# Layer 0's pooled rows and gates transposed on VectorE instead of through DRAM, the block writes moved to ScalarE's queue, and two output columns opened early, in a two-layer fp32 decoder trunk

## The chip, the cores and the metric

One Trainium2 chip, of which one core is used. The metric is the device time of one execution in microseconds (us). The engines are called PE (TensorE, the matmuls), PEld (its weight loads), DVE (VectorE), ACT (ScalarE), POOL (GpSimd) and SP (SyncE, which here only issues DMAs). A queue name such as SPq or ACTq is the DMA queue that this engine fills; an engine works through its instructions strictly in order, so one that waits holds up all behind it.

## The reference

256 positions of width 2048, one batch, all in fp32. What bears on the change is layer 0 and the way that layer 1 gets its queries:

```python
def pool_layer(x, mem, norm_g, w_in, w_pool, pool_scale, mem_g, w_mem_kv, w_out):
    h = rmsnorm(x, norm_g)
    u, zu, qm, zm = jnp.split(h @ w_in, [POOL_W, 2 * POOL_W, 2 * POOL_W + MEM_W], axis=-1)
    y_pool = multiscale_pool(u, w_pool, pool_scale) * jax.nn.silu(zu)
    y_mem = memory_attention(qm * HEAD_DIM ** -0.5, mem, mem_g, w_mem_kv) * jax.nn.silu(zm)
    return x + jnp.concatenate([y_pool, y_mem], axis=-1) @ w_out
```

`multiscale_pool` cuts the 1536 channels of u into four groups of 384. In group g each channel becomes its trailing mean over 2, 4, 8 or 16 positions minus the position's own value; then a 384x384 matrix per group mixes the channels and a scale per channel follows. Layer 1 projects queries, gates and memory queries out of the new stream, attends over compressed, selected and windowed keys (12 heads in four groups of three), mixes the branches and projects out.

## The kernel before, in words

**Products.** Every product is fp32 made of three passes: a number is split into a high part that the matmul keeps exactly (ACT casts it, L138 or L142) and the rest (DVE subtracts, L139 or L143), and `mm3` (L147 to L149) sums high by high, high by low and low by high. `project` (L168) multiplies the stream (stationary, transposed, two blocks of 128 positions) by a weight matrix. It goes in chunks of two k-tiles, 128 x 2 x 384 or 128 x 2 x 512 weights. A chunk is one load on SP's queue into a `raw` tile (four of them), one cast on ACT and one subtraction on DVE into a `w` tile (four of them), and 12 matmuls. After each chunk `project` calls `pump`, which advances the oldest generator of a queue of background work by one step; `flush` runs that queue empty.

**Order.** The source order is only a wish: a scheduler that works with its own price list sets the final order on every engine, and that order is fixed when the program runs.

**Transposes.** A projection leaves rows (positions on the partitions). Where channels must be on the partitions, `turned` (L116 to L128) does it in three steps: two DVE stream transposes turn every 32 x 32 block in place (tile `nt`, L121), one DMA on SP's queue writes `nt` to DRAM (`bnc`, L123), and four DMAs on SP's queue read the blocks back in their new places (tile `tt`, L127). The first waits for DVE, the other four wait until `bnc` has landed.

**Layer 0 around the change.** For each group g of four: project u (384 columns, 8 chunks), scale the rows (ACT, L230), turn; start the background work `pooled` (L465: shifted sums `pt` at L474 and L475, the mean at L481, its split `dd`); project the gate (8 chunks), SiLU (ACT, L236), turn; run `pooled` to its end (`flush(pl)`); start the background work `mixed` (L489: two pool weight loads, 27 matmuls into the PSUM tiles `mix`, and for each of three blocks `yf` at L501, which needs the turned gate). The 18 matmuls of the first two blocks go to one PSUM tile, the 9 of the third to another.

**Output projection of layer 0** (L536 to L550): four columns of 512, each 8 chunks. Column 0 multiplies the six chunks whose inputs are ready, flushes the queue, and then the last two. Each finished column is added to x (L547), turned, and split into layer 1's input `h1`.

**Layer 1**: for the groups 3, 0, 1, 2, `project_q` and `project_gate` (8 chunks each) put turned tiles into `qns` and `gns`; the generator `nsa_heads` (L680) takes them as soon as `ready` (L798) sees them, splits a head's query (`q<-tt`, ACT and DVE), and computes scores (`sc`), softmax, transposes and outputs.

Of the kernel before, what the change touches and what calls it, by code (L numbers as in the profile page):

```python
# [20 lines left out]
P = 128  # L21
# [44 lines left out]
def tile_trunk(ctx, tc, x, mem, xt, memt, positions, w_mem_kv, w_out, a_w_in, a_w_pool, b_w_in, w_kv, cmp_w1, cmp_w2,  # L66
# [22 lines left out]

    bg = deque()  # L90

    def pump():

        while bg:
            try:
                return next(bg[0])
            except StopIteration:
                bg.popleft()
# [17 lines left out]
    def turned(nat, n):  # L116


        nt = wk.tile([P, 4, 2, HD], F32, name="nt", tag="nat", bufs=5)[:, 0:n]
        for t in range(2):  # L120
            V.transpose(nt[:, :, t, :], nat[:, t, 0:n * HD].rearrange("p (h d) -> p h d", d=HD))  # L121
        d = dr.tile([8, P, HD], F32, name="bnc", tag="bnc", bufs=4)[0:2 * n]
        nc.sync.dma_start(d.rearrange("a p d -> p a d"), nt.rearrange("p h t d -> p (h t) d"))  # L123
        tt = wk.tile([P, 4, S], F32, name="tt", tag="nat", bufs=5)[:, 0:n]
        dv = d.rearrange("a (i r) (j c) -> j r (a i) c", r=32, c=32)
        for j in range(4):
            nc.sync.dma_start(tt[32 * j:32 * j + 32].rearrange("r h (i c) -> r (h i) c", c=32), dv[j])  # L127
        return tt  # L128

    def pst(name):  # L130
# [334 lines left out]
    def pooled(g, ut, ds_):  # L465

        def temp():
            return wk.tile([P, 928], F32, name="pt", tag="pm", bufs=2)

        win = POOL_WINDOWS[g]  # L470
        a = ut
        for sh in (1, 2, 4, 8)[:g + 1]:
            b = temp()[:, 0:768].rearrange("p (c s) -> p c s", c=3)
            V.tensor_copy(b[:, :, 0:sh], a[:, :, 0:sh])  # L474
            V.tensor_tensor(out=b[:, :, sh:S], in0=a[:, :, sh:S], in1=a[:, :, 0:S - sh], op=ALU.add)  # L475
            a = b
            yield
        fac = cst[:, C_FAC + 16 * g:C_FAC + 16 * g + win].unsqueeze(1).to_broadcast([P, 3, win])
        V.tensor_tensor(out=a[:, :, 0:win], in0=a[:, :, 0:win], in1=fac, op=ALU.mult)
        d = temp()[:, 0:768].rearrange("p (c s) -> p c s", c=3)  # L480
        V.scalar_tensor_tensor(d, a, 1.0 / win, ut, op0=ALU.mult, op1=ALU.subtract)  # L481
        dd = wk.tile([P, 1536], F32R, name="dd", tag="late", bufs=1)
        dd = [dd[:, 768 * i:768 * i + 768].rearrange("p (c s) -> p c s", c=3) for i in range(2)]
        yield
        split(*dd, d)
        ds_.append(dd)
        yield

    def mixed(g, sg, ds_):  # L489

        wpv = a_w_pool[0, g].rearrange("(a p) n -> p a n", p=P)
        wps = wload(wpv[:, 0:2, :]), wload(wpv[:, 2:3, :])
        yield
        ps = pst("mix")
        for b in range(3):
            o = ps[:, b * S:(b + 1) * S] if b < 2 else pst("mix")[:, 0:S]
            for c in range(3):
                mm3(o, [z[:, c % 2, b * P:(b + 1) * P] for z in wps[c // 2]], [z[:, c, :] for z in ds_[0]], c == 0, c == 2)
            k = 3 * g + b
            y = wk.tile([P, S], F32, name="yf", tag="yf", bufs=1)  # L500
            V.scalar_tensor_tensor(y, o, psc[:, k:k + 1], sg[:, b, :], op0=ALU.mult, op1=ALU.mult)  # L501
            A.copy(y0[k][0], y)
            G.tensor_tensor(out=y0[k][1], in0=y, in1=f32(y0[k][0]), op=ALU.subtract)
            yield

    for g in range(4):
        ut = turned(rows_scaled(project(a_w_in[0], 384 * g, 384, x0), rx, 384), 3)
        if g == 0:
            flush()
            later(rotary_tables())  # L510
        ds_ = []
        pl = later(pooled(g, ut, ds_))
        sg = turned(silu_gate(project(a_w_in[0], 1536 + 384 * g, 384, x0), rx, 384), 3)
        flush(pl)
        later(mixed(g, sg, ds_))

    h1d = dr.tile([S, D], F32, name="h1d")
# [11 lines left out]
    def h1_T(xr, c):  # L529
        yield  # L530
        for j in range(2):
            k = 4 * c + 2 * j
            two_T(xr, 2 * j, h1[k:k + 2])
            yield

    for c in range(4):  # L536
        n_ = slice(c * 512, (c + 1) * 512)
        if c == 0:
            pp = project(w_out[0], 0, 512, y0, groups=[6, 7, 0, 1, 2, 3], done=False)
            flush()  # L540
            pp = project(w_out[0], 0, 512, y0, groups=[4, 5], pp=pp)
        else:
            pp = project(w_out[0], c * 512, 512, y0)
        xr = natural()
# [135 lines left out]
    def nsa_heads():  # L680
# [115 lines left out]
        todo = [(g, h) for g in (3, 0, 1, 2) for h in range(3)]  # L796

        def ready(i, what):  # L798
            while i < len(todo) and todo[i][0] not in what:
                yield  # L800

        yield from ready(0, qns)
        qs[todo[0]] = q_T(qns[todo[0][0]], todo[0][1])
        yield
        for i in range(len(todo) + 1):
            if i < len(todo):
# [1 line left out]
            yield  # L808
            if i + 1 < len(todo):
                yield from ready(i + 1, qns)  # L810
                qs[todo[i + 1]] = q_T(qns[todo[i + 1][0]], todo[i + 1][1])
            if i:
                yield from ready(i - 1, gns)
                gt[todo[i - 1]] = gns[todo[i - 1][0]][:, todo[i - 1][1], :]
            yield
            if i:
                transposed(*todo[i - 1])
# [9 lines left out]
    def project_q(g):  # L827
# [8 lines left out]
                V.tensor_scalar(gc, gc, cst[:, C_RV + t:C_RV + t + 1], None, op0=ALU.mult)  # L836
        qn = rows_scaled(pq, r1, 384)
        rope(heads(qn, 3), 3, 0, 2)
        qns[g] = turned(qn, 3)

    def project_gate(g):
        gns[g] = turned(silu_gate(project(bw, 1572 + 384 * g, 384, h1, ng[1]), r1, 384), 3)

    for g in (3, 0, 1, 2):
        project_q(g)
# [120 lines left out]
```

## Time and profile before

| what | value |
|---|---|
| runs of the kernel, us | 875.3, 881.72, 882.1 (median 881.72) |
| the profiled execution, us | 875.92 |
| its span, first to last instruction, us | 874.1 |
| around the span, us | 1.8 |
| PE busy, share of the span | 849.9 us, 97% |
| DVE busy | 608.5 us, 70% |
| ACT busy | 539.6 us, 62% |
| mean granted PE clock | 0.994 of full |

A row of instructions in time order reads: start, duration (us), engine, line of the program, operation, output <- inputs, shapes, count, and in brackets the idle time of that engine before it and who ended it. "x2" with 1.03 us is two instructions that together took 1.03 us. A row of waits reads: engine and line that waited, who released it, total us, number of times, longest. Rows of stretches give the length, the busy time of every engine with its count, the granted PE clock, the busy share of the DMA engines and the rate in GB/s.

### The profile page before, as it was taken

The numbers are of one execution on the slowest core, as the hardware profiler recorded it, in microseconds if no ns is written. First come the engines' busy times: TensorE is split into PE (matmuls) and PEld (weight loads), VectorE is DVE, ScalarE is ACT, GpSimd is POOL, SyncE is SP. The second block draws the span as 40 slices with busy tenths as digits, with TensorE's granted clock in tenths as the row PEclk, the third lists the DMA queues.
The fourth block names the chain that finished last, engine by engine and source line by source line (L and its number), as shares of the span: only waits on it lengthen the run. The fifth ranks groups of instructions, "written<-read, shape, count | busy, mean of one in ns | idle before, by whom it ended". The sixth has DMA issues, their size and how long they took to land.

```text
span 874.1 us, 12967 instructions
## 1 busy us (share of the span) xinstructions
PE 849.9 (97%) x4408; PEld 752.4 (86%) x4408; DVE 608.5 (70%) x1261; ACT 539.6 (62%) x1025; POOL 40.2 (5%) x63
## 2 busy tenths in 40 slices
PE   9999999999999999999999999989999999999996
PEld 6888889999999878777888888869999989888786
DVE  6677556867565665457667878857689879887752
ACT  7877646755444454447566667747697868676641
POOL 0000000020101020000000000000000010001000
PEclk9999999999999999999999999999999999999999
DMA  9999978678777789898887786798777766786642
GB/s 311 345 274 288 306 222 192 180 219 225 216 204 226 222 257 269 262 262 268 241 228 205 201 276 227 238 251 226 213 193 208 172 183 153 213 244 223 214 159 96
DMA packets 236058, 199.14 MB, mean 228 GB/s; under 512 B 111576, under 2 KB 186328, under 8 KB 235992
## 3 DMA queue, kind: packets, MB, share of 16 engines
q1 hardware_dynamic: 234696, 195.55, 76.9%
q0 software_dynamic: 576, 2.10, 0.6%
q8 instruction: 34, 0.56, 0.3%
q10 hardware_dynamic: 720, 0.67, 0.2%
q14 instruction: 32, 0.26, 0.1%
HBM read 180.99 MB, written 17.30 MB: 227 GB/s over the span
## 4 chain that ended last, share of the span: by engine, by line
PE 60%; DMA 18%; DVE 9%; SPq 4%; ACT 4%; issue 4%; DVEq 0%; POOLq 0%; POOL 0%; ACTq 0%
PE pp L148 18%; PE pp L149 18%; PE pp L147 18%; DMA bnc<-nt 7%; SPq L127 4%; DMA raw<-in_w_out_dram 3%; DMA tt<-bnc 3%; DVE w L139 2%; DMA raw<-in_b_w_in_dram 2%; DVE w L143 1%; DVE nt L121 1%; PE hp L602 1%; DVE pt L475 1%; ACT w L142 1%; ACT pm L714 1%
## 5 line engine op out<-in xcount | busy, mean ns | idle before, releaser
L139 DVE SCALAR_TENSOR_TENSOR w<-raw,fst,w 128x512 fp32r<-128x512 f32 (+2 forms) x320 | 210.5, 699 | 52.7 <-ACT w L138 51.9
L143 DVE TENSOR_TENSOR w<-raw,w 128x1024 fp32r<-128x1024 f32 (+2 forms) x170 | 181.7, 1076 | 92.7 <-ACT w L142 91.1
L138 ACT ACTIVATE w<-raw,fst 128x512 fp32r<-128x512 f32 (+2 forms) x320 | 199.0, 675 | 64.8 <-PE pp L149 31.1
L142 ACT CAST w<-raw 128x1024 fp32r<-128x1024 f32 (+2 forms) x170 | 155.4, 923 | 130.1 <-PE pp L149 66.8
L148 PE MATMUL pp<-w,h1h 128*128 128x512 f32 (+2 forms) x512 | 187.4, 366 | 0.3 <-DVE w L139 0.3
L149 PE MATMUL pp<-w,h1l 128*128 128x512 f32 (+2 forms) x512 | 187.7, 367 | 0.0
L147 PE MATMUL pp<-w,h1h 128*128 128x512 f32 (+2 forms) x512 | 178.8, 367 | 3.0 <-ACT w L138 3.0
L148 PE MATMUL pp<-w,x0h 128*128 128x384 f32 (+1 forms) x320 | 111.2, 348 | 0.0
L149 PE MATMUL pp<-w,x0l 128*128 128x384 f32 (+1 forms) x320 | 111.0, 347 | 0.0
L147 PEld LDWEIGHTS pp<-w,h1h 128*128 128x128 f32 x512 | 96.2, 188 | 13.7 <-ACT w L138 3.8
L147 PE MATMUL pp<-w,x0h 128*128 128x384 f32 (+1 forms) x320 | 107.7, 348 | 0.0
L148 PEld LDWEIGHTS pp<-w,h1h 128*128 128x128 f32 x512 | 96.6, 189 | 10.9 <-DVE w L139 1.1
L149 PEld LDWEIGHTS pp<-w,h1l 128*128 128x128 f32 x512 | 96.6, 189 | 10.3
L148 PEld LDWEIGHTS pp<-w,x0h 128*128 128x128 f32 x320 | 60.5, 189 | 2.8 <-DVE w L143 0.3
L149 PEld LDWEIGHTS pp<-w,x0l 128*128 128x128 f32 x320 | 60.5, 189 | 2.5
L147 PEld LDWEIGHTS pp<-w,x0h 128*128 128x128 f32 x320 | 59.9, 189 | 2.6
L148 PE MATMUL pp<-w,y0h 128*128 128x512 f32 x128 | 50.2, 392 | 1.7 <-DVE w L143 1.7
L148 PE MATMUL pp<-w,mth 128*128 128x512 f32 x128 | 50.3, 393 | 0.1
L149 PE MATMUL pp<-w,mtl 128*128 128x512 f32 x128 | 50.0, 391 | 0.0
L149 PE MATMUL pp<-w,y0l 128*128 128x512 f32 x128 | 49.9, 390 | 0.0
L147 PE MATMUL pp<-w,y0h 128*128 128x512 f32 x128 | 48.7, 390 | 0.1
L147 PE MATMUL pp<-w,y1h 128*128 128x512 f32 (+1 forms) x128 | 46.0, 366 | 0.8 <-DVE nat L869 0.8
(287 smaller groups left out, 1219.8 us busy)
## 6 DMA issues: line engine op xcount, KB each, us to landing
raw<-in_w_out_dram SPq DMA_DIRECT2D x60, 512.0 KB, 5.2
raw<-in_a_w_in_dram SPq DMA_DIRECT2D x64, 384.0 KB, 3.9
raw<-in_w_kv_dram SPq DMA_DIRECT2D x48, 512.0 KB, 4.8
raw<-in_b_w_in_dram SPq DMA_DIRECT2D x56, 384.0 KB, 3.9
raw<-in_w_mem_kv_dram SPq DMA_DIRECT2D x31, 512.0 KB, 5.8
raw<-in_a_w_in_dram SPq DMA_DIRECT2D x16, 512.0 KB, 4.9
raw<-in_b_w_in_dram SPq DMA_DIRECT2D x16, 512.0 KB, 4.9
raw<-in_cmp_w_dram SPq DMA_DIRECT2D x16, 512.0 KB, 4.8
```

The costliest lines, as they stand in the source:

```text
L121: V.transpose(nt[:, :, t, :], nat[:, t, 0:n * HD].rearrange("p (h d) -> p h d", d=HD))
L127: nc.sync.dma_start(tt[32 * j:32 * j + 32].rearrange("r h (i c) -> r (h i) c", c=32), dv[j])
L138: A.activation(hi, src, AF.Copy, scale=scale)
L139: V.scalar_tensor_tensor(lo, src, scale, f32(hi), op0=ALU.mult, op1=ALU.subtract)
L142: A.copy(hi, src)
L143: V.tensor_tensor(out=lo, in0=src, in1=f32(hi), op=ALU.subtract)
L147: T.matmul(o, s[0], m[0], start=start, stop=False, **kw)
L148: T.matmul(o, s[0], m[1], start=False, stop=False, **kw)
L149: T.matmul(o, s[1], m[0], start=False, stop=stop, **kw)
L475: V.tensor_tensor(out=b[:, :, sh:S], in0=a[:, :, sh:S], in1=a[:, :, 0:S - sh], op=ALU.add)
L602: T.matmul(hp, zs[:, l].rearrange("p i g n -> p (i g n)"), wb[:, :, a * 256:(a + 1) * 256], start=l == 0, stop=l == 31)
L714: A.activation(pm[:, o:o + n], pm[:, o:o + n], AF.Exp, bias=mx[:, t, b:b + 1], scale=SCALE, accum_out=su[:, t, b:b + 1])
```

## The change

Five things change.

1. `turned` issues the write of `bnc` from ACT's queue instead of SP's (all 21 tiles that still use it).
2. A new `turned_here` replaces `turned` for the eight tiles of layer 0's groups (four pooled inputs, four gates): sixteen DVE stream transposes of 32 partitions each put every 32 x 32 block at its place at once, 192 elements per partition in each, with no DMA.
3. In layer 0 `pooled` waits four steps before its first sum, `mixed` one step before its loads, and `flush(pl)` is gone, so `pooled` may run on into the next projection.
4. The output projection of layer 0 opens columns 0 and 1 with six chunks each before the flush, then closes 0, then 1.
5. Layer 1's heads take a turned tile only six pump steps after it was issued (`ticks`).

```diff
         d = dr.tile([8, P, HD], F32, name="bnc", tag="bnc", bufs=4)[0:2 * n]
-        nc.sync.dma_start(d.rearrange("a p d -> p a d"), nt.rearrange("p h t d -> p (h t) d"))
+        nc.scalar.dma_start(d.rearrange("a p d -> p a d"), nt.rearrange("p h t d -> p (h t) d"))
...
+    def turned_here(nat, n):
+
+        tt = wk.tile([P, 4, S], F32, name="th", tag="nat", bufs=5)[:, 0:n]
+        src = nat[:, :, 0:n * HD].rearrange("p t (h j c) -> p h t j c", j=4, c=32)
+        to = tt.rearrange("p h (t i c) -> p h t i c", t=2, c=32)
+        for j in range(4):
+            for i in range(4):
+                V.transpose(to[32 * j:32 * j + 32, :, :, i, :], src[32 * i:32 * i + 32, :, :, j, :])
+        return tt
...
         a = ut
+        for _ in range(4):
+            yield
         for sh in (1, 2, 4, 8)[:g + 1]:
...
         wpv = a_w_pool[0, g].rearrange("(a p) n -> p a n", p=P)
+        yield
         wps = wload(wpv[:, 0:2, :]), wload(wpv[:, 2:3, :])
...
-        ut = turned(rows_scaled(project(a_w_in[0], 384 * g, 384, x0), rx, 384), 3)
+        ut = turned_here(rows_scaled(project(a_w_in[0], 384 * g, 384, x0), rx, 384), 3)
...
-        pl = later(pooled(g, ut, ds_))
-        sg = turned(silu_gate(project(a_w_in[0], 1536 + 384 * g, 384, x0), rx, 384), 3)
-        flush(pl)
+        later(pooled(g, ut, ds_))
+        sg = turned_here(silu_gate(project(a_w_in[0], 1536 + 384 * g, 384, x0), rx, 384), 3)
...
+    opened = []
     for c in range(4):
         n_ = slice(c * 512, (c + 1) * 512)
         if c == 0:
-            pp = project(w_out[0], 0, 512, y0, groups=[6, 7, 0, 1, 2, 3], done=False)
+            for c_ in range(2):
+                opened.append(project(w_out[0], c_ * 512, 512, y0, groups=[6, 7, 0, 1, 2, 3], done=False))
             flush()
-            pp = project(w_out[0], 0, 512, y0, groups=[4, 5], pp=pp)
+        if c < 2:
+            pp = project(w_out[0], c * 512, 512, y0, groups=[4, 5], pp=opened[c])
...
-            while i < len(todo) and todo[i][0] not in what:
+
+            while i < len(todo) and (todo[i][0] not in what or ticks[0] < what[todo[i][0]][1] + 6):
                 yield
```

Where the compiled order moves, at the three places that the prediction speaks of.

DVE, layer 0, the end of a gate projection of the third group (g = 2; `w` is a chunk's split, the `w` of 128x384 the second pool weight, `nt` the two transposes of the gate, `yf` the gated output). Before:

```order
L481 SCALAR_TENSOR_TENSOR pt<-pt,tt 128x768
L143 TENSOR_TENSOR w<-raw,w 128x384
L143 TENSOR_TENSOR dd<-pt,dd 128x768
L121 STREAM_TRANSPOSE nt<-nat 128x3x128 x2
L143 TENSOR_TENSOR w<-raw,w 128x768 x3
L501 SCALAR_TENSOR_TENSOR yf<-mix,fst,tt 128x256
```

Now (`th` is the tile that the sixteen transposes write):

```order
L156 TENSOR_TENSOR dd<-pt,dd 128x768
L156 TENSOR_TENSOR w<-raw,w 128x768
L140 STREAM_TRANSPOSE th<-nat 32x6x32 x16
L156 TENSOR_TENSOR w<-raw,w 128x768
L156 TENSOR_TENSOR w<-raw,w 128x384
L156 TENSOR_TENSOR w<-raw,w 128x768 x2
L517 SCALAR_TENSOR_TENSOR yf<-mix,fst,th 128x256
```

Sixteen instructions in a row stand where two stood, ahead of the next chunk's split and of the pool weight's; `yf` reads `th`, which DVE itself wrote, and no longer `tt`, which four DMAs wrote.

SP's queue, the output projection of layer 0 (`nat<-in_x` is the load of x for a finished column). Before:

```order
L123 DMA bnc<-nt 128x8x128
L156 DMA raw<-in_w_out_dram 128x2x512 x2
L127 DMA tt<-bnc 32x32x32 x4
L545 DMA nat<-in_x_dram 128x2x512
L156 DMA raw<-in_w_out_dram 128x2x512 x6
```

Now:

```order
L169 DMA raw<-in_w_out_dram 128x2x512 x18
L130 DMA tt<-bnc 32x32x32 x4
L563 DMA nat<-in_x_dram 128x2x512
L169 DMA raw<-in_w_out_dram 128x2x512 x6
L130 DMA tt<-bnc 32x32x32 x4
L563 DMA nat<-in_x_dram 128x2x512
L169 DMA raw<-in_w_out_dram 128x2x512 x3
```

From one read-back of a column to the next there were eight weight loads before (six and two), and there are six now.

ACT, layer 1, from the first query tile (`nat`) to its first use (`q`); each "x2" of `w` is one chunk's cast. Before:

```order
L230 ACTIVATE nat<-pp_5352,r_3711 128x384
L138 ACTIVATE w<-raw,fst 128x384 x14
L142 CAST q_5563<-tt 128x256
```

Now:

```order
L243 ACTIVATE nat<-pp_5408,r_3767 128x384
L151 ACTIVATE w<-raw,fst 128x384 x6
L126 DMA bnc<-nt 128x6x128
L151 ACTIVATE w<-raw,fst 128x384 x6
L155 CAST q_5714<-tt 128x256
```

Six chunks' casts stand between the tile and its use where seven stood, and the write to DRAM waits on ACT for the two transposes.

## Rows read from the trace of the kernel before

**Rows 1.** The page: span, and busy time of each engine.
```profile
span 874.1 us, 12967 instructions
PE 849.9 (97%) x4408; PEld 752.4 (86%) x4408; DVE 608.5 (70%) x1261; ACT 539.6 (62%) x1025; POOL 40.2 (5%) x63
```

**Rows 2.** Waits of PE, the two largest kinds of the whole run.
```profile
PE sc L147 <- ACT q L142: 3.7, 3, 1.9
...
PE pp L147 <- ACT w L138: 3.3, 3, 2.8
```

**Rows 3.** Waits of PE between 196 and 330 us (layer 0's groups).
```profile
PE mix L147 <- DVE yf L501: 3.4, 3, 1.8
PE pp L148 <- DVE w L143: 1.2, 2, 0.7
PE mix L148 <- DVE dd L143: 0.5, 1, 0.5
```

**Rows 4.** PE in time order, 226 to 233 us.
```profile
226.36 0.34 PE L149 MATMUL pp<-w,x0l 128*128 128x384 f32 x1
228.46 0.39 PE L147 MATMUL mix<-dd,w 128*128 128x256 f32 x1 [1.76 <-DVE yf L501]
...
230.67 0.52 PE L148 MATMUL pp<-w,x0h 128*128 128x384 f32 x1
```

**Rows 5.** DVE groups, forms apart, between 196 and 312 us.
```profile
L143 DVE TENSOR_TENSOR w<-raw,w 128x768 fp32r<-128x768 f32 x43 | 42.3, 991 | 21.6 <-ACT w L142 21.2
L121 DVE STREAM_TRANSPOSE nt<-nat 128x384 f32<-128x384 f32 x12 | 6.3, 560 | 0.6 <-ACT nat L230 0.6
...
L501 DVE SCALAR_TENSOR_TENSOR yf<-mix,fst,tt 128x256 f32<-128x256 f32 x7 | 3.3, 477 | 11.8 <-DMA tt<-bnc 11.8
```

**Rows 6.** DVE in time order, at three pairs of transposes.
```profile
199.71 1.10 DVE L121 STREAM_TRANSPOSE nt<-nat 128x384 f32<-128x384 f32 x2 [0.31 <-ACT nat L230]
...
216.87 1.03 DVE L121 STREAM_TRANSPOSE nt<-nat 128x384 f32<-128x384 f32 x2
...
325.24 1.29 DVE L121 STREAM_TRANSPOSE nt<-nat 128x512 f32<-128x512 f32 x2
```

**Rows 7.** ACT in time order, 198 to 201 us.
```profile
199.09 1.10 ACT L230 ACTIVATE nat<-pp,rx 128x384 f32<-128x384 f32 x2 [0.68 <-PE pp L149]
200.09 0.82 ACT L142 CAST w<-raw 128x768 fp32r<-128x768 f32 x1
```

**Rows 8.** Stretches: from:to, length, PE, PEld, DVE, ACT, POOL, clock, DMA share, GB/s.
```profile
190.00:220.00 30.00, 30.00 (x182) 30.00 (x182) 22.14 (x30) 16.49 (x24) 2.75 (x3) 1.00 0.79 222
220.00:250.00 30.00, 28.24 (x158) 27.92 (x157) 14.43 (x18) 12.68 (x18) 3.09 (x3) 0.94 0.77 204
250.00:280.00 30.00, 28.24 (x169) 27.49 (x168) 21.13 (x30) 14.57 (x22) 3.10 (x3) 1.00 0.74 218
280.00:312.00 32.00, 30.76 (x166) 27.53 (x164) 18.28 (x27) 12.42 (x17) 0.74 (x1) 1.00 0.81 231
...
200.00:210.00 10.00, 10.00 (x60) 10.00 (x59) 4.78 (x8) 4.26 (x6) 0.00 (x0) 1.00 0.86 217
```

**Rows 9.** SP's queue in time order, the first output column of layer 0.
```profile
326.56 0.37 SPq L123 DMA_DIRECT2D bnc<-nt  x1
327.66 1.59 SPq L156 DMA_DIRECT2D raw<-in_w_out_dram  x2
332.23 4.64 SPq L127 DMA_DIRECT2D tt<-bnc  x4
...
337.52 10.21 SPq L156 DMA_DIRECT2D raw<-in_w_out_dram  x6
349.78 0.37 SPq L123 DMA_DIRECT2D bnc<-nt  x1
```

**Rows 10.** PE and ACT in time order, at the first and third query tile.
```profile
632.69 0.71 ACT L142 CAST q<-tt 128x256 fp32r<-128x256 f32 x2 [3.21 <-DMA tt<-bnc]
...
633.15 0.39 PE L147 MATMUL sc<-kn,q 128*128 128x272 f32 x1 [0.52 <-ACT q L142]
...
714.83 0.40 ACT L142 CAST q<-tt 128x256 fp32r<-128x256 f32 x1 [3.89 <-DMA tt<-bnc]
```

More of the change, by code (lines that the diff above doesn't have):

```diff
@@ L90, in tile_trunk @@
     bg = deque()
+    ticks = [0]
     def pump():
+        ticks[0] += 1
         while bg:
@@ L798, in ready @@
         def ready(i, what):
-            while i < len(todo) and todo[i][0] not in what:
+            while i < len(todo) and (todo[i][0] not in what or ticks[0] < what[todo[i][0]][1] + 6):
                 yield
         yield from ready(0, qns)
-        qs[todo[0]] = q_T(qns[todo[0][0]], todo[0][1])
+        qs[todo[0]] = q_T(qns[todo[0][0]][0], todo[0][1])
         yield
@@ L810, in nsa_heads @@
                 yield from ready(i + 1, qns)
-                qs[todo[i + 1]] = q_T(qns[todo[i + 1][0]], todo[i + 1][1])
+                qs[todo[i + 1]] = q_T(qns[todo[i + 1][0]][0], todo[i + 1][1])
             if i:
                 yield from ready(i - 1, gns)
-                gt[todo[i - 1]] = gns[todo[i - 1][0]][:, todo[i - 1][1], :]
+                gt[todo[i - 1]] = gns[todo[i - 1][0]][0][:, todo[i - 1][1], :]
             yield
@@ L838, in project_q @@
         rope(heads(qn, 3), 3, 0, 2)
-        qns[g] = turned(qn, 3)
+        qns[g] = turned(qn, 3), ticks[0]
     def project_gate(g):
-        gns[g] = turned(silu_gate(project(bw, 1572 + 384 * g, 384, h1, ng[1]), r1, 384), 3)
+        gns[g] = turned(silu_gate(project(bw, 1572 + 384 * g, 384, h1, ng[1]), r1, 384), 3), ticks[0]
     for g in (3, 0, 1, 2):
```

## The prediction

> **What bounds the kernel now.** I read the page first: PE is busy 849.9 of 874.1 us [rows 1], so the matmuls themselves set the time and no change around them can win more than the 24.2 us in which PE stands idle, plus what a lowered PE clock costs. So the next view is the list of what PE waits for. Over the whole run the largest kinds are the scores that wait for a split query (3.7 us in three waits) and chunks that wait for a cast (3.3 us, of which 2.8 us is one wait) [rows 2]. In layer 0's groups the third `mix` block waits for `yf` (3.4 us in three waits), `mix` for `dd` (0.5 us), and chunks for DVE's split (1.2 us) [rows 3], together 5.1 us. The reader should see there that DVE and ACT, 70% and 62% busy [rows 1], matter only where PE stands behind them.
>
> The cause of the `mix` waits is the way through DRAM: DVE stood idle 11.8 us ahead of its seven `yf`, all of it until `tt` landed [rows 5]. The time order of PE shows one of them, 1.76 us, and after it matmuls of 128x384 that take 0.52 us instead of 0.34 [rows 4]. There the granted clock has fallen to its lower level, 1.2 GHz instead of 2.4: the stretch from 220 to 250 us has a mean clock of 0.94 [rows 8], which costs 30 x 0.06 = 1.8 us. PE had been idle just before it fell.
>
> **The change part by part.**
>
> *The way through DRAM goes, for eight tiles.* It takes away the late `tt` and with it all waits of [rows 3], 5.1 us, and the fall of the clock that followed the first, 1.8 us: -6.9 us. The order supports it: `yf` now reads what DVE itself wrote, sixteen moves that stand ahead of it in the order. The wait for `dd` goes because `mixed` loads one step later, and the three waits of the last group (the 1.2 us among them) because two output columns are opened before the flush, twelve chunks of PE work instead of six. What stays is at least 0 and at most all of it, so the term lies between 0 and -6.9; I take the whole, since the work that now lies between the gate and its use is nearest to the rows without a wait.
>
> *Sixteen transposes on DVE, eight times.* A pair of 128x384 takes 1.03 us when both follow on other work, and one of them alone 0.56 [rows 5, 6]; so the second starts 1.03 - 0.56 = 0.47 us after the first. A pair of 128x512 takes 1.29 [rows 6], 0.26 more for twice 128 elements, so an element costs about 1.0 ns. A move of 192 elements then starts 0.47 - 0.195 = 0.275 us after the one before and lasts 0.56 - 0.195 = 0.365. Sixteen: 15 x 0.275 + 0.365 = 4.5 us, against 1.03 now: 3.5 us more per tile, 28 us of DVE in all. DVE was busy 76 of the 122 us from 190 to 312 [rows 8]; with 28 more it is at 85%, still under PE. So what counts is not the sum but the block: for 4.5 us DVE splits no weights.
>
> What covers a block is the store of split chunks. The order puts three chunks ahead of it. PE makes 60 matmuls in 10 us there [rows 8], so a chunk of 12 is 2.0 us and three are 6.0. The scaling of the first half ran at 199.09, released by PE's last matmul of that half [rows 7], three matmuls or 0.5 us before PE is through with the chunk, so the new projection starts near 199.5. The fourth chunk's low part is wanted after 6.0 us and two matmuls that need only its high part (0.3): at 205.8. DVE can begin when both halves are scaled, at 200.2 [rows 7], ends the block at 204.7 and the split, 0.99 us [rows 5], at 205.7. It just fits. I take 0.25 us late for each of the four pooled inputs, 1.0 us; the four gates I cost at nothing, because the 18 `mix` matmuls lie in PE's order after the three chunks and hide it. If that cover fails they cost the same, 1.0 more. The bounds of the move are its elements alone (0.2 us, 3.2 a block, nothing late) and the full 128x384 price of 0.47 (7.6 a block, rival two).
>
> *The waits of the queue.* SP issues eight writes and 32 reads less; that frees the weight loads behind them in layer 0's groups, where DMA is 74% to 81% busy [rows 8], and I cost it at 0, since no PE wait of [rows 3] is on a load. The writes that remain move to ACT's queue, where each waits for two transposes; behind it stand the next chunk's cast and all after it. ACT is hidden by the same store of chunks. Between 0 and 1 us each if it were not; I take 0, since on SP, too, the column's write waited for its transposes and went out 0.03 us after them (325.24 + 1.29 = 326.53 against 326.56) [rows 6, 9].
>
> *Output columns.* Opening column 1 early brings the first two columns' results closer together: six weight loads of SP stand between one read-back and the next, instead of eight. SP was busy or blocked with a read-back from 329.25 to 336.87 (the end of the two loads before it to the end of the four reads), 7.6 us, then 0.6 for x; six loads take 10.2 us [rows 9]. Before, 8 x 1.7 + 8.2 = 21.8 us for eight chunks, about the 23.2 us from one write to the next [rows 9]. Now 10.2 + 8.2 = 18.4 us for six chunks, which at the same rate are 17.4, less what PE no longer waits, some 16.3. So the queue falls short by up to 2.1 us in each of two periods. Bounds 0 and 4.2; I take 2.0, as the first twelve chunks run without a read-back and fill the store.
>
> *Six steps for the heads.* By the order the queries' casts move from 7, 21, 38 and 53 chunks to 6, 23, 37 and 55. ACT waited 3.21 us for the first and 3.89 for the third tile [rows 10]. Where the cast comes a chunk earlier nothing lands sooner: the first score, which waited 0.52 us [rows 10], now waits up to 2 us more, and the third tile keeps its wait, on PE or as a cast held up behind it. The second and fourth lose theirs, some 1.3 us. Sum: 0, bounds -3.7 (all of [rows 2]) and +3. The last heads end about a chunk later; the projection of the other column covers that.
>
> **Sum.** -6.9 + 1.0 + 2.0 + 0 = -3.9 us. The profiled execution took 874.1 + 1.8 = 875.9 us, so 872.0. The runs shown are 875.3, 881.7 and 882.1, median 881.7; the profiled one lies with the lowest. I carry half of the 5.8 us between it and the median: 872.0 + 2.9 = 874.9, 0.8% under the median.
>
> **The rivals.**
>
> *One: the full gain.* Nothing is late, the queue keeps up and the query waits go too: 875.9 - 6.9 - 3.7 + 2.9 = 868.2 us. For it speaks that the changes aim at each wait that the list names; against it that two of four query casts come earlier, not later, and that the store just fits.
>
> *Two, slower: the block outlasts the store.* Place: DVE, between the third and the fourth chunk after each projection of layer 0. If a move of 32 partitions costs what one of 128x384 does, 0.47 us, a block is 15 x 0.47 + 0.56 = 7.6 us, the fourth chunk is 200.2 + 7.6 + 0.99 - 205.8 = 3.0 us late, eight times 24 us: 874.9 - 1.0 + 24 = 897.9. It is slower by over 1% from 890.5 us, that is from 2.1 us late, a block of 6.7 us or 0.42 us per move. Against it: the price rose with the elements from 384 to 512 [rows 6].
>
> *Three: no overlap of the moves.* If a move begins only when the one before is out, it costs its whole 0.365 us: 5.8 a block, 1.2 late, eight times 9.6: 874.9 - 1.0 + 9.6 = 883.5, no change. Against it: two transposes took 1.03 us and one 0.56 [rows 5, 6], so 0.09 overlapped. The Trainium skill, "VectorE: DVE Perf Modes", section "The DRAIN you can't avoid", says that the next operation of this engine does not start before the pipeline of the one before has emptied, and so speaks for few large operations; by that rule the time is this rival's, and the trace agrees only in part (0.47 of 0.56).
>
> *Four: the waits come back elsewhere.* The change does not do what it says: `yf` stands behind splits that wait for PE, the read-backs of the output columns fall short by the whole 4.2 us, PE idles and the clock falls once more (1.8): 874.9 + 2.2 + 1.8 = 878.9, and 885.8 if the 6.9 stay as well. For it speaks that DMA-bound waits move easily; against it the order of `yf`.
>
> **How the numbers follow.** Forecast 0.44, one 0.26, two 0.09, three 0.09, four 0.12. A difference of 1% (8.8 us: under 872.9 or over 890.5) is about what a measurement of this kernel can tell from no change. Faster: all of one and a quarter of the forecast, whose own range is 870 to 880: 0.36. Slower: two and a share of four: 0.13. The rest is the same: 0.51. Range 864 to 889: it holds the forecast, one, three and four, and cuts two.
>
> **What would show it.** In the profile after, `th` moves with a mean near 0.37 us and sixteen in about 4.5; no PE wait `mix` for `yf`; clock near 1.00 between 220 and 250; PE waits for `w` under 0.5 us after each block. A mean of 0.5 us or a wait of 1 us or more after each block would prove two or three, and PE waits on `w` around the columns or the first scores would prove four. The forecast is wrong if PE's idle time falls by over 8 us or not at all.

## The result and the profile after

The changed kernel took 892.0 us (median of 4 runs, 890.4 to 892.8) against 881.2 for the kernel before on the same chip (875.3 to 882.1): ratio 1.014, 95% interval 1.011 to 1.017. A later measurement on another chip gave 1.0156 (1.010 to 1.021). So it is slower by more than 1%, where the prediction said no change, and its 892 us lie above the range. The profiled execution took 891.88 us, 16.0 more than the one of before.

The chips differ: on them the kernel before took 875 to 881 us. Below, a kernel is therefore given by its ratio to the kernel before on the same chip, and 0.1% is 0.9 us.

The page after, span and busy time of each engine:

```profile
span 890.1 us, 13014 instructions
PE 850.7 (96%) x4408; PEld 753.1 (85%) x4408; DVE 646.1 (73%) x1373; ACT 540.2 (61%) x1025; POOL 39.0 (4%) x63
```

PE does the same work as in [rows 1]; DVE does 646.1 - 608.5 = 37.6 us more. The span has grown by 16.0 us, nearly all of it idle time of PE. Not all of that lies where the prediction looked: PE's last matmul of layer 0's output projection starts at 389.26 us before and at 396.15 now, 6.9 us later, and its last matmul of all 16.0 us later, so 9 of the 16 us come in layer 1. The waits of PE, whole run (total, times, longest):

```profile
PE pp L161 <- DVE w L156: 10.1, 8, 2.5
PE pp L160 <- ACT w L151: 5.2, 4, 4.0
PE sc L160 <- ACT q L155: 5.0, 2, 2.5
PE mix L162 <- DVE w L156: 2.2, 2, 1.1
PE pp L160 <- ACT y1h L270: 2.0, 1, 2.0
...
PE o_n L161 <- DVE late L156: 1.0, 1, 1.0
...
PE o_n L160 <- DVE yf L269: 0.6, 1, 0.6
...
PE o_n L160 <- ACT late L155: 0.4, 1, 0.4
```

Held against [rows 2] and [rows 3]: the waits of `mix` for `yf` and for `dd` are gone, as meant. In their place 12.3 us of waits for a split `w` stand at the top. The wait for ACT's `w` rose from 3.3 to 5.2 us, that for `q` from 3.7 to 5.0. The kind with `y1h` and the last three shown, 4.0 us together, are not in the list of before at all; all four lie after 822 us.

Three of the waits for `w`, and then the longest one, with DVE's rows and PE's:

```profile
191.05 0.44 PE L161 MATMUL pp<-w,x0h 128*128 128x384 f32 x1 [1.70 <-DVE w L156]
...
232.25 0.39 PE L162 MATMUL mix<-dd,w 128*128 128x256 f32 x1 [1.10 <-DVE w L156]
...
253.50 0.44 PE L161 MATMUL pp<-w,x0h 128*128 128x384 f32 x1 [1.59 <-DVE w L156]
```

```profile
206.57 6.12 DVE L140 STREAM_TRANSPOSE th<-nat 32x192 f32<-32x192 f32 x16
212.73 2.70 DVE L156 TENSOR_TENSOR w<-raw,w 128x768 fp32r<-128x768 f32 x3
```

```profile
210.73 0.51 PE L160 MATMUL pp<-w,x0h 128*128 128x384 f32 x2
213.74 0.45 PE L161 MATMUL pp<-w,x0h 128*128 128x384 f32 x1 [2.50 <-DVE w L156]
```

Sixteen moves take 6.12 us, not 4.5. The three chunks split ahead are used up at 211.2; DVE is through at 212.7, needs one split more, and PE starts again at 213.7. Behind the pooled inputs' four blocks `pp` waits 0.6, 2.5, 1.6 and 1.6 us, 6.3 together; behind the gates' `pp` waits 1.7 and 0.6 (first and fourth) and `mix` 1.1 twice (second and third), 4.6 together. The moves by form and the stretches, DVE and all engines, in layer 0:

```profile
L140 DVE STREAM_TRANSPOSE th<-nat 32x192 f32<-32x192 f32 x96 | 35.5, 370 | 4.0 <-ACT nat L243 1.6 <-ACT nat L249 1.2
```

```profile
190.00:220.00 30.00, 26.45 (x159) 26.13 (x160) 23.87 (x42) 11.96 (x19) 4.21 (x4) 1.00 0.55 177
220.00:250.00 30.00, 28.90 (x175) 28.58 (x174) 23.54 (x44) 15.68 (x23) 3.13 (x3) 1.00 0.60 179
250.00:280.00 30.00, 27.27 (x164) 26.63 (x164) 25.96 (x48) 12.60 (x18) 0.74 (x1) 1.00 0.52 159
280.00:312.00 32.00, 30.41 (x164) 28.59 (x163) 29.45 (x57) 15.13 (x22) 1.89 (x2) 1.00 0.60 196
```

A move lasts 0.370 us, as worked out (0.365), but sixteen of them in 6.12 us start (6.12 - 0.37) / 15 = 0.383 us apart, where the prediction had 0.275. DVE is busy 102.8 of the 122 us, 84%, as expected; PE stands idle 9.0 us there, against 4.8 in [rows 8]. The clock is at 1.00 throughout, where it was 0.94 from 220 to 250 us: that gain came. It was lost again behind layer 0: the mean from 700 to 780 us is 0.98, where it was 1.00, and over the whole run it is 0.992 against 0.994.

### The profile page after: what moved, and what is told of

Read it like the earlier page. It is cut to its first block, busy times and chain, and to the rows that moved or that the text cites. A ratio compares the mean times of both kernels' runs of the same rounds, so it can differ in the third digit from the quotient of the medians.

```text
span 890.1 us, 13014 instructions
## 1 busy us (share of the span) xinstructions
PE 850.7 (96%) x4408; PEld 753.1 (85%) x4408; DVE 646.1 (73%) x1373; ACT 540.2 (61%) x1025; POOL 39.0 (4%) x63
## 4 chain that ended last, share of the span: by engine, by line
PE 48%; DMA 18%; DVE 15%; ACT 9%; issue 6%; SPq 3%; POOL 0%; ACTq 0%; DVEq 0%; POOLq 0%
PE pp L161 14%; PE pp L162 14%; PE pp L160 14%; DMA bnc<-nt 5%; DVE th L140 4%; DMA raw<-in_w_kv_dram 3%; SPq L130 3%; DVE w L152 3%; ACT w L151 2%; DMA raw<-in_w_out_dram 2%; DMA tt<-bnc 2%; DVE w L156 2%; DMA raw<-in_w_mem_kv_dram 2%; ACT w L155 2%; DMA nat<-in_x_dram 1%
## 5 line engine op out<-in xcount | busy, mean ns | idle before, releaser
L155 ACT CAST w<-raw 128x1024 fp32r<-128x1024 f32 (+3 forms) x170 | 155.7, 923 | 139.8 <-PE pp L162 65.2
L156 DVE TENSOR_TENSOR w<-raw,w 128x1024 fp32r<-128x1024 f32 (+3 forms) x170 | 180.6, 1078 | 81.2 <-ACT w L155 80.7
L161 PE MATMUL pp<-w,x0h 128*128 128x384 f32 (+1 forms) x320 | 111.3, 348 | 8.5 <-DVE w L156 8.5
L160 PE MATMUL pp<-w,x0h 128*128 128x384 f32 (+1 forms) x320 | 103.5, 346 | 0.1
L140 DVE STREAM_TRANSPOSE th<-nat 32x192 f32<-32x192 f32 x128 | 47.3, 370 | 5.3 <-ACT nat L243 1.9
```

Source lines behind the costliest of these rows:

```text
L140: V.transpose(to[32 * j:32 * j + 32, :, :, i, :], src[32 * i:32 * i + 32, :, :, j, :])
L155: A.copy(hi, src)
L156: V.tensor_tensor(out=lo, in0=src, in1=f32(hi), op=ALU.subtract)
L160: T.matmul(o, s[0], m[0], start=start, stop=False, **kw)
L161: T.matmul(o, s[0], m[1], start=False, stop=False, **kw)
```

## The experiments

Two questions: what the moves cost and why (theories M, B, S against E), and what the smaller parts of the change do (T, Q, N).

### What the moves cost

**The way through DRAM in the changed kernel (e1_dram).**

```diff
-        ut = turned_here(rows_scaled(...), 3)
+        ut = turned(rows_scaled(...), 3)
-        sg = turned_here(silu_gate(...), 3)
+        sg = turned(silu_gate(...), 3)
```

> The changed kernel, with layer 0's pooled rows and gates turned by the way through DRAM again; the rest of the change stays. Theory M (the moves): each of the 128 moves starts 0.38 us after the one before, a block of sixteen takes 6.1 us, and DVE splits no weights for that long; PE's waits on the split `w` after each block (10.1 us in 8 in the trace after) are then gone, and the time is 10 us or so lower, 880 to 884 us, if the way through DRAM brings 0 to 3 us of waits for `yf` of its own. Theory E (elsewhere: the columns opened early, the six steps, the write on ACT's queue): the time stays within 3 us of the changed kernel's, 889 to 895.

Measured: 1.0035 (1.0007 to 1.0064), in us 877.8 on a chip where the kernel before takes 875.1. The moves cost the changed kernel 1.014 - 1.0035, about 1.1% or 9 us, which is theory M. PE's waits from 150 to 336 us:

```profile
PE mix L160 <- DVE yf L517: 2.0, 2, 1.2
PE pp L161 <- DVE w L156: 0.7, 2, 0.4
```

2.7 us, with the way through DRAM, against 5.1 in [rows 3]: the new order of steps alone takes away half of the waits that the prediction put down to DRAM.

**The moves alone in the kernel before (e2_here).** Edit: `turned_here` added to the kernel before and called for layer 0's eight tiles, nothing else.

> The kernel before, with only the eight tiles turned by sixteen moves of DVE; order of steps, write queue, columns and heads as before. Theory M: the `yf` waits of before (5.1 us) go, and waits of about 1.2 us after each block, eight or seven times, come in: 881 - 5 + 10 = 886 us, 884 to 890. Theory E: nothing is lost to the blocks, and the time is 876 to 881.

Measured: 1.0269 (1.0234 to 1.0303), 22 us slower by the medians, far more than theory M said. The waits for `w` from 150 to 336 us, and PE in time order at the longest of them:

```profile
PE pp L158 <- DVE w L153: 20.5, 8, 5.1
```

```profile
316.53 0.39 PE L159 MATMUL pp<-w,y0l 128*128 128x512 f32 x1
...
322.68 0.80 PE L158 MATMUL pp<-w,y0h 128*128 128x512 f32 x1 [5.08 <-DVE w L153]
323.28 0.63 PE L159 MATMUL pp<-w,y0l 128*128 128x512 f32 x1
```

Four of the eight come behind the pooled inputs' blocks, 0.6 us once and 1.24 three times, and four behind the gates', 3.6 to 5.1 us; there PE had the `mix` matmuls behind it already. Behind the longest stop the same matmul takes 0.63 us instead of 0.39: the clock is at its lower level, 1.2 GHz instead of 2.4. From 150 to 336 us its mean is 0.94; what that costs can't be read off as 0.06 x 186 = 11 us, since part of the low stretch is the stop itself: over the whole run PE is busy 852.1 us, only 2.2 more than before, and idle 41.4 instead of 24.2. The stops make the difference. The same blocks cost the changed kernel 1.1%, so the rest of the change holds their price down; which part of it does was not tried apart.

**The changed kernel again (e5_after), and the price of a move (e7_price).** The edit of e7: the pooled rows' moves in the order j = (i + s) mod 4, so that neighbours share no 32 partitions; the gates' moves in halves.

```diff
-        for j in range(4):
+        for s in range(4):
             for i in range(4):
-                V.transpose(to[32 * j:32 * j + 32, :, :, i, :], src[32 * i:32 * i + 32, :, :, j, :])
+                j = (i + s) % 4 if not halves else s
+                for t in (range(2) if halves else [slice(None)]):
+                    V.transpose(to[32 * j:32 * j + 32, :, t, i, :], src[32 * i:32 * i + 32, :, t, j, :] if halves else src[32 * i:32 * i + 32, :, :, j, :])
```

> The changed kernel as it stands, on the chip on which the runs of this set are timed, so that they can be held against it directly. Both theories expect its ratio to the kernel before to be 1.014 within 0.003, and on DVE again 128 moves of 0.37 us that start 0.38 us apart.

> One look at the price of a move. The pooled rows' sixteen moves run in another order, so that no move reads or writes the 32 partitions that the one before it did; the gates' moves are cut in halves of 96 elements, 32 of them. If a move begins only when the one before is out, as the trace after shows (0.38 us apart, 0.37 long), the pooled block stays at 6.1 us; if it is the shared 32 partitions that keep two moves apart, the spacing falls to about 0.28 us and the block to 4.6. For the halves: at 1.0 ns an element, as 0.56 - 0.37 us for 192 elements says, a half lasts 0.27 us, and the gates' block takes 32 x 0.28 = 9 us; if the price were by the element alone, 6.1 us.

Measured: e5 1.0156 (1.0099 to 1.0213), as expected. e7, one execution, DVE in time order: the first gate's block of halves, the second gate's, a pooled block, and the last eighteen halves of the third gate's:

```profile
185.28 0.27 DVE L142 STREAM_TRANSPOSE th<-nat 32x96 f32<-32x96 f32 x1 [0.46 <-ACT nat L251]
185.88 8.51 DVE L142 STREAM_TRANSPOSE th<-nat 32x96 f32<-32x96 f32 x31
...
232.52 7.92 DVE L142 STREAM_TRANSPOSE th<-nat 32x96 f32<-32x96 f32 x32 [0.64 <-ACT nat L251]
...
255.55 6.13 DVE L142 STREAM_TRANSPOSE th<-nat 32x192 f32<-32x192 f32 x16 [0.61 <-ACT nat L245]
...
278.10 4.11 DVE L142 STREAM_TRANSPOSE th<-nat 32x96 f32<-32x96 f32 x18
```

Shared partitions are not what keeps two moves apart: the pooled block stays at 6.13 us. A half lasts 0.27 us, so a move costs about 0.17 us and 1.0 ns an element. But the halves do overlap in part. The first gate's block takes the 9 us that were expected without overlap, the other three 7.9. In these the first fourteen start 0.28 us apart; of the last eighteen every second one starts 0.20 us after the one ahead, 0.07 before that one is out (18 in 4.11 us, where 0.28 apart would make 5.0). In the program's order the two halves of a move, which read and write the same 32 partitions, stand next to each other. The two transposes of 128x384 in [rows 6] work on the same partitions too, and they overlap (of the pair at 216.87 us the first lasts 0.57 us and the second starts at 217.36, 0.08 before it is out), while in the program's order each whole move reads other partitions than the one ahead. So a likely rule is that the overlap is lost where the next move reads or writes other partitions. The trace does not record which half is which, so this is not shown. (The whole run, 909.7 us, has 64 instructions more on DVE and is not a version to compare.)

**Blocks or sum (e6_spread, then e13_pinned).** Edit of e6: sixteen moves as a function `moves(j)` of four, called at four steps of `pooled` and, in place of its one step ahead of the loads, of `mixed`.

```diff
-        for _ in range(4):
+        for j in range(4):
+            moves(j)
             yield
...
+        for j in range(4):
+            moves(j)
+            yield
         wpv = a_w_pool[0, g].rearrange("(a p) n -> p a n", p=P)
-        yield
```

> The changed kernel with the same 128 moves, four of them (1.5 us) at each of four steps behind a projection instead of sixteen at once; the number of moves and what they cost is unchanged. Theory B (the block: what hurts is that DVE splits no weights for 6.1 us at a stretch): the waits on the split `w` between 186 and 320 us (10.8 us in 8, `mix` and `pp` together) fall to under 3 us, and the time is 7 to 10 us under the changed kernel's. Theory S (the sum: DVE has too little time left at all, at 155 us busy of 186): the waits move along with the moves and stay at 8 us or more, the time within 3 us of the changed kernel's.

Measured: 1.0123 (1.0063 to 1.0183), no clear difference from the changed kernel, and waits for `w` of 8.7 us in 11 between 150 and 336 us. That looks like theory S. But DVE's rows show that the edit had not done what it said:

```profile
200.94 4.19 DVE L141 STREAM_TRANSPOSE th<-nat 32x192 f32<-32x192 f32 x11 [1.25 <-ACT nat L245]
205.16 0.96 DVE L158 TENSOR_TENSOR w<-raw,w 128x768 fp32r<-128x768 f32 x1
206.15 1.93 DVE L141 STREAM_TRANSPOSE th<-nat 32x192 f32<-32x192 f32 x5
```

The scheduler put the moves together again, eleven and five. So the next run held them in the order of the program:

```diff
-                V.transpose(to[32 * j:32 * j + 32, :, :, i, :], src[32 * i:32 * i + 32, :, :, j, :])
+                pinned(V.transpose(to[32 * j:32 * j + 32, :, :, i, :], src[32 * i:32 * i + 32, :, :, j, :]))
```

> The changed kernel with the same 128 moves dealt out four to a step and held in the order of the program, so that between two groups of four (1.5 us) DVE splits a chunk of weights. Theory B (block): the waits on `w` between 186 and 320 us fall from 10.8 us to under 4, and the time is 6 to 10 us under the changed kernel's, ratio 1.004 to 1.008. Theory S (sum): DVE has 8 splits of 0.9 and 6.1 us of moves and 3 to 5 us of pooling against 16.6 us of a projection on PE, which it can hold only with nothing lost; the waits stay at 8 us or more, the ratio between 1.011 and 1.016.

Measured: 1.0033 (1.0016 to 1.0049), 879.2 us. Theory B: the moves are the same 128, and 1.1 to 1.2% is gone; it is a little under the expected ratio. The later loads of `mixed` are not the reason, since e6 has them too. DVE in time order, the same stretches as above, and the only wait for `w` from 150 to 336 us:

```profile
209.07 0.96 DVE L158 TENSOR_TENSOR w<-raw,w 128x768 fp32r<-128x768 f32 x1
210.06 1.52 DVE L141 STREAM_TRANSPOSE th<-nat 32x192 f32<-32x192 f32 x4
211.60 0.96 DVE L158 TENSOR_TENSOR w<-raw,w 128x768 fp32r<-128x768 f32 x1
212.59 1.52 DVE L141 STREAM_TRANSPOSE th<-nat 32x192 f32<-32x192 f32 x4
```

```profile
190.00:220.00 30.00, 29.05 (x176) 28.66 (x176) 24.11 (x45) 14.35 (x21) 2.21 (x3) 1.00 0.57 169
220.00:250.00 30.00, 30.00 (x183) 30.00 (x183) 26.29 (x48) 14.88 (x21) 2.70 (x3) 1.00 0.68 200
250.00:280.00 30.00, 30.00 (x180) 29.91 (x179) 26.98 (x48) 13.72 (x20) 1.39 (x2) 1.00 0.58 190
280.00:312.00 32.00, 32.00 (x161) 28.37 (x160) 30.68 (x52) 17.09 (x20) 1.69 (x2) 1.00 0.71 238
```

```profile
PE pp L163 <- DVE w L158: 1.0, 1, 1.0
```

DVE is busier than in the changed kernel (108.1 of 122 us, 89%), and PE is busy 121.0 us of them instead of 113.0. A group of four and a split take 1.52 + 0.96 = 2.5 us, 0.5 more than PE's 2.0 for a chunk; by that estimate four such groups use up 2 us of the store of 6, not all of it.

**The gates back through DRAM (e8_gates_dram).** Edit: `sg = turned(...)`, the pooled inputs as in the changed kernel.

> The changed kernel with the four gates turned by the way through DRAM again, the four pooled inputs by moves of DVE. Theory B: the waits ahead of `mix` and behind it that the gates' blocks make (1.2 us each, four times or so) go and the pooled inputs' stay (1.8 to 2.7 us, four times): 3 to 5 us under the changed kernel's time, less up to 2 us if `yf` waits for `tt` again. A rival, that the gates are free since 18 `mix` matmuls cover them, as the prediction had it: within 2 us of the changed kernel's, or above it.

Measured: 1.0142 (1.0087 to 1.0197). No gain that can be told from the changed kernel (892.6 against 892.8 us on the same chip): the rival's number, though intervals of 5 us don't exclude theory B's 3. The rival's reason does not hold: the changed kernel's trace has 4.6 us of waits behind the gates' blocks, and here nearly all of them are gone. One of the pooled inputs' waits is now 4.9 us instead of 2.5, and `yf` and a `w` behind it bring 1.0, so in this trace another wait takes most of what the gates leave. Why that one grew stayed open.

### What the smaller parts do

**The six steps for the heads (e3_noticks, e10_ticks).** Edits: `+ 6` removed from `ready` in the changed kernel; the tick counter and the six steps alone put into the kernel before.

> The changed kernel without the six steps that a head waits for its turned query or gate. Theory M: the steps are small beside the moves; the time is within 2 us of the changed kernel's. Theory E with the steps as its place: the first score's wait (2.7 us against 0.7 before) and the stops of the last heads between 821 and 830 us (4.7 us) go back, and the time is 3 to 6 us lower, 886 to 889.

> The kernel before with the six steps alone. Theory T: the heads end later, the stops of the last head (`o_n` for `late`, `pA` and `yf`, `pp` for `y1h`) appear after 800 us, and the time is 2 to 6 us over the kernel before, ratio 1.002 to 1.007. Rival N: ratio between 0.997 and 1.002, the waits for `q` lower by as much as the tail's rise.

Measured: e3 1.0149 (1.0118 to 1.018), no gain (its 887.0 us lie in theory E's range only because its chip is the fastest). e10 1.0059 (1.0033 to 1.0085), 5 us slower. Waits of PE after 800 us, in e10:

```profile
PE o_n L150 <- ACT late L145: 2.9, 1, 2.9
PE o_n L151 <- DVE late L146: 1.0, 1, 1.0
PE o_n L150 <- DVE yf L259: 0.6, 1, 0.6
```

4.5 us where the kernel before has 0.8, and the mean clock from 780 to 820 us is 0.91 instead of 1.00 (at most 0.09 x 40 = 3.6 us). That is theory T: the last head ends behind the chunks that should cover it, and its chain of short steps stands bare. In e3 the tail has no such wait, as theory T says, but its time is the changed kernel's: in its trace the first attention score still waits 2.2 us and `pp` for ACT's `w` 6.4 us, more than the 5.2 after. The gain of 3 to 6 us did not come there.

**One column opened early (e4_onecol).** Edit: `range(1)` for `range(2)`, `c < 1` for `c < 2`.

> The changed kernel with one output column of layer 0 opened ahead of the flush instead of two. Theory M: within 2 us of the changed kernel's, up to 1 us slower since the last group's `mix` has less work of PE to hide behind. Theory E with the columns as its place: 2 to 4 us lower, 888 to 890, since SP's queue has eight loads between one read-back and the next again.

Measured: 1.0177 (1.0147 to 1.0206), not lower. In the traces the waits from 336 to 440 us are 2.6 us with two early columns, 2.3 with one and 1.2 before. No loss through the second column can be told; if anything it helps.

**The queue of the writes (e11_spq, e9_dram_noticks, e12_dram_spq).** Edit of e11: `nc.sync.dma_start` for the write in `turned`. e9 is e1 without the six steps, e12 is e9 with the write on SP's queue.

> The changed kernel with the writes to DRAM on SP's queue again. Theory Q (on ACT's queue a write goes out beside SP's loads instead of between them and lands later: near 573 us SP sat from 573.1 to 580.0 before it could read back, 6.9 us, against 5.15 in the kernel before, and PE's stop behind it grew from 2.9 to 4.2 and 5.3 us): that stop falls to 3 us or less, and the time is 1 to 3 us under the changed kernel's, ratio 1.011 to 1.014. Rival N: the queue of the write matters nothing, ratio within 0.002 of 1.0148, the mean of the two measurements of the changed kernel.

> The changed kernel with layer 0's eight tiles turned by the way through DRAM and without the six steps for the heads; the new order of layer 0 and the two output columns opened early remain, and the write on ACT's queue. Theory T (the steps push the last heads behind the last chunks of the output projections, where nothing covers them: PE stops of 4 to 8 us after 756 us in each kernel with the steps, none or one in those without): the tail's stops go, part of it comes back in the heads' stage, and the time is 2 to 6 us under that of the kernel with the steps and the way through DRAM (ratio 1.0035), so 0 to 4 us under the kernel before. Rival N (the steps only move waits about): the ratio stays between 1.000 and 1.006.

> As the first of this set (way through DRAM, no steps for the heads), and with the writes on SP's queue too: what is left of the change is the new order of layer 0 and the two columns opened early. Theories T and Q together: below the first by up to 2 us and below the kernel before by 3 to 7 us, ratio 0.992 to 0.997, by the stops of layer 0 (4.0 us before, 3.4 in the kernel with the way through DRAM) and of the output columns (2.7 before, none there). If neither holds: 0.998 to 1.003.

Measured: e11 1.0138 (1.0103 to 1.0172), which decides nothing between Q and N; e9 1.0007 (0.9981 to 1.0034), 0.3% under e1, the low end of theory T but within rival N's range too, and the two intervals overlap; e12 0.9947 (0.992 to 0.9974), within what T and Q together expect and faster than the kernel before. e9 and e12, timed on the same chip, differ by the queue alone: 0.6%, 5 us. One place shows it, layer 1's `kv` stage. The write in e9, then SP's queue and PE's wait; then the same of e12:

```profile
562.16 0.37 ACTq L126 DMA_DIRECT2D bnc<-nt  x1
```

```profile
564.37 0.37 SPq L169 DMA_DIRECT2D raw<-in_w_kv_dram  x1
568.70 2.58 SPq L130 DMA_DIRECT2D tt<-bnc  x4
```

```profile
580.85 1.22 PE L160 MATMUL pp<-w,h1h 128*128 128x512 f32 x2 [5.27 <-ACT w L151]
```

```profile
562.22 0.37 SPq L126 DMA_DIRECT2D bnc<-nt  x1
...
567.01 4.23 SPq L130 DMA_DIRECT2D tt<-bnc  x4
```

```profile
578.15 0.73 PE L160 MATMUL pp<-w,h1h 128*128 128x512 f32 x2 [2.29 <-ACT w L151]
```

From the write to the read-back it is 6.5 us on ACT's queue and 4.8 on SP's; SP waits that long with the weight loads behind it, and PE's wait for a chunk is 3.0 us shorter in e12. Why the write takes longer on ACT's queue there is not shown. The same write in the changed kernel takes 6.9 us (573.63 to 580.54) and in the kernel before 5.15. In e11 too it takes 4.9, and PE's stop behind it falls from 4.0 us in the changed kernel to 2.1, as theory Q said; but `o_n` now waits 3.1 us for `late` instead of 0.4, and the time did not fall clearly. It is this one place and no general gain: the next write of the stage is read back 3.8 us later in e9 and 4.1 in e12, and over all 29 writes the times from write to read-back add up to 123 us on ACT's queue and 120 on SP's. The other 2 us of e9 against e12 I have not located.

**The moves beside the best rest (e15_moves_rest, e14_pinned_rest).** Edits: the changed kernel without the six steps and with the write on SP's queue, once with the sixteen moves together (e15), once with four pinned to a step (e14). Their partner with the way through DRAM is e12.

> The changed kernel without the six steps and with the writes on SP's queue; the sixteen moves stand together as in the changed kernel. Its partner has the way through DRAM in their place and the ratio 0.9947. Both theories: the moves cost what they cost with the steps and ACT's queue, 1.1%, so 1.004 to 1.009; a rival, that the moves cost more here since nothing else hides behind their waits: over 1.010.

> As the first of this set, and without the six steps and with the writes on SP's queue. Theory B: near the kernel with the way through DRAM and the same rest (ratio 0.995), 0.993 to 1.000. Theory S: 1.003 to 1.009, since the moves cost 8 us or more there as well.

Measured: e15 1.0091 (1.0068 to 1.0114): the blocks cost 1.0091 - 0.9947 = 1.4% there (e12 was timed on another chip), a little over the 1.1% expected. e14 0.9932 (0.9912 to 0.9952), 869.7 us against 876.3: faster than both kernels, 6.5 us under the kernel before. On one chip e15 and e14 differ by 13.5 us, through the dealing out (with the later loads of `mixed`) and the pinning alone. This is the cleanest measure of the blocks. From e12 (0.9947) e14 can't be told apart, so the moves as such bring nothing that can be told over the way through DRAM. Its longest waits of PE:

```profile
PE sc L162 <- ACT q L157: 5.1, 3, 2.6
PE pp L162 <- ACT w L153: 2.6, 2, 2.0
PE pp L163 <- DVE w L158: 1.9, 2, 1.0
```

What remains above all is the queries that wait for their read-back, as in [rows 10].

## Why the prediction was wrong

- **"The way through DRAM goes": -6.9 us, mechanism right.** The waits of [rows 3] went, and so did the fall of the clock there. But half of those waits goes with the order of steps alone (e1: 2.7 us left). Order and early columns together make e12 0.5%, 4 to 5 us, faster than the kernel before, and its trace has 4.3 of them by the end of layer 0's output projection (384.99 us instead of 389.26).
- **"A move of 192 elements then starts 0.275 us after the one before": the term that failed.** The 0.365 us of one move was right (0.370); the overlap, read from two transposes of 128x384, does not hold for these moves of 32 partitions, which start 0.383 us apart. (It was read as 0.09 from a mean of 0.56; row by row it is 0.08 at most.) The block is 6.1 us instead of 4.5. The working behind it stands: with 6.1 it gives 200.2 + 6.1 + 0.99 - 205.8 = 1.5 us late, and behind the pooled inputs the trace has 1.6 twice (0.6 at the first, where the moves do not stand in one block); where it has 2.5, DVE stood at a `yf` behind POOL and began the block 1.1 us after its rows were scaled (205.4). The late blocks were put at 1.0 us in all; the waits for `w` of layer 0 are 10.8 us (8.6 of `pp` and 2.2 of `mix`, 150 to 336 us), and e1 shows some 9 us, e14 against e15 13.5. This is rival three's mechanism, put at 0.09, and nearly its cost (9.6 us). Rival three still said no change; that the kernel is slower by more than 1% took the queue and the steps as well, by the ratios below.
- **"The four gates I cost at nothing": wrong.** 4.6 us of waits stand behind their blocks. At two gates `mix` itself stood for `w`, 1.1 us each: its own weights are split by the same DVE, so it can't cover the block. What the gates cost the whole run e8 left open.
- **The rule of the Trainium skill ("VectorE: DVE Perf Modes", section "The DRAIN you can't avoid") that the next operation of this engine does not start before the pipeline of the one before has emptied.** For the whole moves the trace agrees: 0.383 us apart and 0.370 long. For the halves of e7 it agrees in part: 29 of 128 begin 0.07 us before the one ahead is out. The same passage says that an operation which is not held starts earlier; the prediction left that out. I weighed the rule against one pair of another shape and took the pair.
- **"The queue waits": 0.** Wrong in kernels with the way through DRAM: 5 us (e9 against e12), of which 3.0 are located. In the changed kernel itself the time shows no difference (e11), though the stop at the `kv` stage is 1.9 us shorter there.
- **"Output columns": +2.0.** No loss can be told (e4). The changed kernel, e1 and e12 have 1.8 to 2.6 us of waits in the columns' stage (336 to 440 us), the kernel before 1.2.
- **"Six steps": 0, bounds -3.7 to +3.** Alone they cost 5 us (e10; 2.9 to 7.4), above the bound. That "the projection of the other column covers that" is what failed: 4.0 us of waits after 822 us in the changed kernel. Taking them out of it brought no gain by itself (e3).

One way from the kernel before to the changed one, by the ratios: order and early columns -0.5% (e12), moves in blocks +1.4% (e15 against e12), write queue and six steps together +0.5 to +0.65% (the changed kernel against e15). So the blocks are the largest term that failed, and the queue and the steps, both put at 0, the second. The traces agree: without queue and steps (e15) the loss in layer 1 is 3.0 us instead of 9. Taken singly in the changed kernel neither of the two shows in its time (e3, e11); in other surroundings each cost 0.3 to 0.6% (e9, e10). How they add up is therefore not shown.

## What to carry to other kernels

Price a block by the spacing of just such instructions, not by the overlap of larger ones, and where it only just fits behind a store of prepared work, take the rival without the overlap for the likelier. A busy share of 84% or 89% says nothing about such a block: cut into pieces shorter than one round of the consumer, and pinned so that the scheduler cannot join them again, the same instructions were nearly free. (Nearly free is not a gain: the kernel with pinned moves and the one with the way through DRAM can't be told apart.) Delaying short chained work "until its data is surely there" costs time at the end of the program, where nothing is left to cover it.

## What the runs showed of the hardware

- A stream transpose of 32 partitions lasts about 0.17 us and 1.0 ns an element of a partition (0.370 us for 192 elements, 0.27 for 96). Whole moves, each of which reads other 32 partitions than the one ahead, start 0.383 us apart, without overlap. Two of 128x384 in a row overlap by up to 0.08 us, and 29 of e7's 128 halves by 0.07 us with the half ahead.
- At one place of the `kv` stage a write to DRAM issued from ACT's queue was read back 5.7 to 8.6 us later (ten kernels; 6.9 in the changed one), the same write on SP's queue 4.8 to 5.2 us later (seven). At the next write of the stage it is the other way round (3.8 us in e9, 4.1 in e12).
- Stops of PE of 3.8 and 5.1 us were followed by matmuls at the lower clock in e2 (behind the longer one 0.63 us instead of 0.39); after stops of 1.70 and 2.50 us in the changed kernel's layer 0 the granted clock stayed at 1.00. The length of the stop alone does not tell: in the kernel before, the clock fell after one of 1.76 us [rows 4].
